# The low parts of eight weight pieces made by a negated copy on ScalarE and an accumulating transfer

## The chip, the cores and the metric

The kernel runs on one core of one Trainium2 chip. A core has TensorE (PE), VectorE (DVE), ScalarE (ACT), GpSimd (POOL) and SyncE (SP), each with a queue of its own that it works through in order, and DMA engines that all queues share. The metric is the device time of one execution in microseconds; less is better. Before the change it is 1096.87 us, the median of three runs (1096.74 to 1097.33).

## The reference

The reference is a network of two layers on 256 tokens with 1024 features, in float32. Each layer has a feed-forward block, a mixer and another feed-forward block; every one is normed, modulated by a vector c, and added to x. The first layer's mixer is the hybrid: a gated linear recurrence (LRU) beside a state-space part (SSD).

```python
for layer in range(DEPTH):
    mod = (c_act @ ada_w[layer] + ada_b[layer]).reshape(bsz, N_SUB, 3, D_MODEL)[:, :, :, None, :]
    ...
    h = modulate(x, 0)
    x = x + HALF_STEP * (1.0 + mod[:, 0, 2]) * swiglu(h, ffn_w_gate[layer, 0], ffn_w_up[layer, 0], ffn_w_down[layer, 0])
    h = modulate(x, 1)
    if layer % 2 == 0:
        ...
        y = hybrid_mixer(h, hyb_w_in[e], hyb_w_out[e], lru_conv_w[e], lru_conv_b[e], ...)
    else:
        ...
        y = mlstm_block(h, mlstm_w_up[o], ...)
    x = x + (1.0 + mod[:, 1, 2]) * y.astype(x.dtype)
    ...
return rms_norm(x, final_norm_g)
```

In the hybrid, `h @ w_in` gives five parts: the gate and the input of the LRU, and z, xbc and dt of the SSD. A causal convolution of width 4 runs over the LRU's input and over xbc. The outputs of both parts are put beside each other and multiplied by `w_out`.

## The kernel before

**Weights as a stream of pieces.** All large weights lie in DRAM as one list of 128x128 tiles in the order in which TensorE uses them, eight tiles to a piece: 366 pieces of 128x1024 in float32, 512 KB each. TensorE multiplies in a rounded format (float32r), so a weight is split into a high part, the rounded weight, and a low part, what the rounding left out; the activations are split the same way. A product is then three matmuls: high weight by high activation (L443), high by low (L444), low by high (L445). In `begin`, which starts a block ahead of its norm, the same three are L509 to L511.

**How a piece is made.** `_piece` (L91 on) loads the raw piece by a transfer of SP (L95), lets ACT round it to `whi` by a copy (L101), and DVE subtract to give `wlo` (L102). Edges of the form "in order" keep ACT's copies in the order of the pieces, and DVE's subtractions too. `behind` sets a piece's copy or subtraction behind another instruction; in the hybrid this concerns pieces 70 to 72. `W.last` is the newest subtraction; `pump` (L273 on) sets the blocks of the modulation (one transfer of SP and one DVE instruction of 128x1024 each, L260 and L262) behind it.

**Buffers.** There are four raw buffers. `whi` and `wlo` have three places each by the piece's number modulo 3, two buffers to a place, so that a piece's parts go where those of the piece six earlier were. `next` makes pieces four ahead of the one that TensorE begins (`LEAD`).

**The hybrid.** It is made of pieces 66 to 119. Pieces 66 to 69 are the first four chunks of xbc, 70 to 77 its other eight (`xbc_pair`, `xbc_rest`); from 78 to 95 a loop takes, by turns, eight tiles of the LRU's input (`xl`), eight of z and two for the LRU's gates (`ri`); 96 to 103 are the LRU's gate (`gl`), and 104 to 119 the output (`od`). Each product fills one of four PSUM banks, which must be read out before it is filled again. For xbc and xl the convolution does that: its first tap by ACT (L730), the other three by DVE (L733). For z, ACT takes a tanh and DVE reads the bank once more (L949, L950); for `ri`, ACT reads both halves (L920, L922).

The SSD's sum runs beside the products of `gl`. For each of four pairs of chunks ACT makes decays (L983, L985, and an exponential, L986), DVE multiplies them (L988, L992), and TensorE uses them (L1008). Twice the norm of four chunks is found from a sum over tokens (L359) and a chain of eight small steps of DVE (L373 to L329) whose end is spread by TensorE (L405).

**What sets the order.** The order of each engine's instructions is the scheduler's of the framework: by priority in the order of the program, with the timing that it assumes, and bound by the edges written by hand. It is fixed when the kernel is built. POOL issues a few small loads and fills a few tiles; in the hybrid its last instructions are two fills (L846, L849) at 192 us.

Of the kernel before, what the change touches and what calls it, by code (L numbers as in the profile page):

```python
# [11 lines left out]
F32 = mybir.dt.float32  # L12
F32R = mybir.dt.float32r
I32 = mybir.dt.int32
AF = mybir.ActivationFunctionType
ALU = mybir.AluOpType
AX = mybir.AxisListType
NOSYNC = mybir.DependencyInfo(mybir.DependencyClass.NoSync, mybir.DependencyReason.DATA)
# [45 lines left out]
WARM = 3  # L64
SUMS = {"n1": (1, 11), "n2": (2, 11), "n4": (4, 14)}
WHOLE = 2


ADA_PLAN = [
# [5 lines left out]
class Weights:  # L75
# [4 lines left out]
    def __init__(self, tc, src, raw_pool, part_pool, pump):  # L80
        self.tc, self.nc, self.src, self.pump = tc, tc.nc, src, pump
        self.raw_pool, self.part_pool = raw_pool, part_pool
        self.pos = 0
        self.made = 0
        self.ahead = 0
        self.parts = {}
        self.products = []
        self.splits = {}
        self.after = {}

    def _piece(self, i):  # L91
        nc = self.nc
        w = PIECE * P
        raw = self.raw_pool.tile([P, w], F32, tag="wraw", name=f"wraw{i}")
        nc.sync.dma_start(raw, self.src[i])  # L95
        if i < WHOLE:
            self.parts[i] = (raw, None)
            return
        hi, lo = (self.part_pool.tile([P, w], F32R, tag=f"{n}{'abc'[i % 3]}", name=f"{n}{i}") for n in ("whi", "wlo"))
        with self.tc.high_priority(offset=self.ahead):  # L100
            raw_hi = nc.scalar.copy(hi, raw)  # L101
            self.last = nc.vector.tensor_tensor(out=lo, in0=raw, in1=hi.bitcast(F32), op=ALU.subtract)  # L102
        if i < 2:
            self.tc.add_manual_dep(self.last.ins, self.first.ins.name, NOSYNC, reason="the first input first")
        self.parts[i] = (hi, lo)
        self.splits[i] = (raw_hi, self.last)
        if i - 1 in self.splits:
            for n in range(2):
                self.tc.add_manual_dep(self.splits[i][n].ins, self.splits[i - 1][n].ins.name, NOSYNC, reason="in order")
        for n, ins in self.after.pop(i, ()):  # L110
            self._behind(i, n, ins)

# [1429 lines left out]
```

## Time and profile before

| what | value |
|---|---|
| median of three runs | 1096.87 us |
| the profiled execution | 1097.25 us |
| its span, first to last instruction | 1095.5 us |
| granted TensorE clock | 0.999 |
| DVE, ACT and POOL busy | 920.5, 639.5 and 8.8 us |
| moved by DMA | 272.34 MB |
| of it by POOL's queue | 1.04 MB in 400 packets |

A row of a group says the line, the engine and the operation, what it writes and reads by the program's names, its shape and count, then busy time, the mean of one in ns, the idle time of the engine just ahead of it and what ended that. A timeline row begins with the start in us from the span's start and the duration. A matmul's row shows 276 ns, but matmuls overlap in the array: how fast TensorE goes is seen from one start to the next. A hole in TensorE's work is therefore read from start to start too; the idle time that the row gives is shorter.

### The profile page before, as it was taken

The numbers are of one execution on the slowest core, as the hardware profiler recorded it, in microseconds if no ns is written. First come the engines' busy times: TensorE is split into PE (matmuls) and PEld (weight loads), VectorE is DVE, ScalarE is ACT, GpSimd is POOL, SyncE is SP. The second block draws the span as 40 slices with busy tenths as digits, with TensorE's granted clock in tenths as the row PEclk, the third lists the DMA queues.
The fourth block names the chain that finished last, engine by engine and source line by source line (L and its number), as shares of the span: only waits on it lengthen the run. The fifth ranks groups of instructions, "written<-read, shape, count | busy, mean of one in ns | idle before, by whom it ended". The sixth has DMA issues, their size and how long they took to land.

```text
span 1095.5 us, 23272 instructions
## 1 busy us (share of the span) xinstructions
PE 1083.8 (99%) x9315; PEld 1070.4 (98%) x9315; DVE 920.5 (84%) x1654; ACT 639.5 (58%) x1053; POOL 8.8 (1%) x28
## 2 busy tenths in 40 slices
PE   9999999999999999999999999999999999999997
PEld 7999999999999999999999999999999999999997
DVE  7999999899999899989698798979768868866552
ACT  5765555678986564554454455448776655544452
POOL 0000000000000000000000000010000000000000
PEclk9999999999999999999999999999999999999999
DMA  9889999556855489999848799963432664875551
GB/s 375 344 318 391 387 352 343 178 196 195 279 167 191 139 307 370 354 351 327 281 142 323 266 356 346 338 204 119 146 102 81 208 193 137 298 239 193 193 174 39
DMA packets 75534, 272.34 MB, mean 249 GB/s; under 512 B 8593, under 2 KB 9393, under 8 KB 75426
## 3 DMA queue, kind: packets, MB, share of 16 engines
q1 hardware_dynamic: 74592, 269.38, 69.7%
q8 instruction: 73, 1.20, 0.4%
q0 software_dynamic: 400, 1.04, 0.4%
q10 hardware_dynamic: 434, 0.43, 0.1%
q14 instruction: 35, 0.29, 0.1%
HBM read 269.77 MB, written 1.05 MB: 247 GB/s over the span
## 4 chain that ended last, share of the span: by engine, by line
PE 80%; DVE 12%; DMA 4%; issue 2%; ACT 1%; ACTq 0%; DVEq 0%; SPq 0%
PE gu L445 12%; PE gu L444 12%; PE gu L443 11%; PE od L445 10%; PE od L443 10%; PE od L444 10%; DVE wlo L102 4%; DMA wraw<-in_wst_dram 3%; PE zz L445 1%; PE zz L443 1%; PE zz L444 1%; DMA wgr<-in_ml_wg_dram 1%; DVE ada L262 1%; DVE xc L733 1%; PE gu_f L509 1%
## 5 line engine op out<-in xcount | busy, mean ns | idle before, releaser
L102 DVE TENSOR_TENSOR wlo<-wraw,whi 128x1024 fp32r<-128x1024 f32 x364 | 442.9, 1221 | 83.6 <-ACT whi L101 83.0
L101 ACT CAST whi<-wraw 128x1024 fp32r<-128x1024 f32 x364 | 378.2, 1050 | 210.9 <-DMA wraw<-in_wst_dram 80.2
L444 PE MATMUL gu<-hb,whi 128*128 128x256 f32 x1296 | 358.0, 276 | 0.4 <-DVE hb L668 0.3
L443 PE MATMUL gu<-hb,whi 128*128 128x256 f32 x1296 | 358.0, 276 | 0.0
L445 PE MATMUL gu<-hb,wlo 128*128 128x256 f32 x1296 | 357.9, 276 | 0.1
L444 PEld LDWEIGHTS gu<-hb,whi 128*128 128x128 f32 x1296 | 243.3, 188 | 0.8 <-DVE hb L668 0.8
L445 PEld LDWEIGHTS gu<-hb,wlo 128*128 128x128 f32 x1296 | 243.3, 188 | 0.2 <-DVE wlo L102 0.2
L443 PEld LDWEIGHTS gu<-hb,whi 128*128 128x128 f32 x1296 | 243.2, 188 | 0.0
L443 PE MATMUL od<-ph,whi 128*128 128x256 f32 x704 | 194.3, 276 | 0.0
L444 PE MATMUL od<-ph,whi 128*128 128x256 f32 x704 | 194.3, 276 | 0.0
L445 PE MATMUL od<-ph,wlo 128*128 128x256 f32 x704 | 194.3, 276 | 0.0
L262 DVE SCALAR_TENSOR_TENSOR ada<-ada,cact 128x1024 f32<-128x1024 f32 x144 | 175.3, 1218 | 1.4 <-DMA ada<-in_adaT_dram 1.3
L444 PEld LDWEIGHTS od<-ph,whi 128*128 128x128 f32 x704 | 132.1, 188 | 0.0
L445 PEld LDWEIGHTS od<-ph,wlo 128*128 128x128 f32 x704 | 132.1, 188 | 0.0
L443 PEld LDWEIGHTS od<-ph,whi 128*128 128x128 f32 x704 | 132.1, 188 | 0.0
L426 ACT CAST ph<-fg 128x256 fp32r<-128x256 f32 x88 | 35.1, 406 | 114.9 <-DVE fg L595 114.9
L427 DVE TENSOR_TENSOR ph<-fg,ph 128x256 fp32r<-128x256 f32 x88 | 36.4, 421 | 14.2 <-ACT ph L426 14.2
L416 ACT ACTIVATE sq_o<-x 128x256 f32<-128x256 f32 x42 | 17.5, 418 | 45.6 <-DVE x L571 40.6
L571 DVE SCALAR_TENSOR_TENSOR x<-od,gate,x 128x256 f32<-128x256 f32 x48 | 23.1, 481 | 24.4 <-PE od L445 24.2
L444 PE MATMUL zz<-hb,whi 128*128 128x256 f32 x128 | 36.2, 283 | 0.0
L445 PE MATMUL zz<-hb,wlo 128*128 128x256 f32 x128 | 36.1, 282 | 0.0
L443 PE MATMUL zz<-hb,whi 128*128 128x256 f32 x128 | 35.8, 279 | 0.0
(431 smaller groups left out, 1959.1 us busy)
## 6 DMA issues: line engine op xcount, KB each, us to landing
wraw<-in_wst_dram SPq DMA_DIRECT2D x366, 512.0 KB, 4.6
ada<-in_adaT_dram SPq DMA_DIRECT2D x144, 512.0 KB, 5.6
xn<-in_x_dram SPq DMA_DIRECT2D x2, 512.0 KB, 4.0
wgr<-in_ml_wg_dram POOLq DMA_DIRECT2D x3, 256.0 KB, 5.4
out_dram<-res SPq DMA_DIRECT2D x3, 128.0 KB, 2.4
out_dram<-res ACTq DMA_DIRECT2D x1, 256.0 KB
out_dram<-res SPq DMA_DIRECT2D x1, 256.0 KB, 2.9
cols<-in_cols_dram SPq DMA_DIRECT2D x1, 190.0 KB, 9.5
```

What stands on the lines that cost most here:

```text
L101: raw_hi = nc.scalar.copy(hi, raw)
L102: self.last = nc.vector.tensor_tensor(out=lo, in0=raw, in1=hi.bitcast(F32), op=ALU.subtract)
L262: return nc.vector.scalar_tensor_tensor(out=raw, in0=raw, scalar=1.0, in1=cact, op0=ALU.mult, op1=ALU.mult, accum_out=mods[s][:, m:m + 1])
L416: square = nc.scalar.activation(q, x, AF.Square).ins
L426: nc.scalar.copy(hi, src)
L427: nc.vector.tensor_tensor(out=both[:, 1, :], in0=src, in1=hi.bitcast(F32), op=ALU.subtract)
L443: m = nc.tensor.matmul(dst, wh, both[:, 0, :], start=start, stop=False, skip_group_check=True)
L444: W.products += [m, nc.tensor.matmul(dst, wh, both[:, 1, :], start=False, stop=False, skip_group_check=True), nc.tensor.matmul(dst, wl, bo ...
L445: nc.tensor.matmul(dst, wl, both[:, 0, :], start=False, stop=stop, skip_group_check=True)]
L509: W.products += [nc.tensor.matmul(dst, wh, rh, start=(k == 0), stop=False), nc.tensor.matmul(dst, wh, rl, start=False, stop=False), nc.ten ...
L571: nc.vector.scalar_tensor_tensor(out=xs_t[d], in0=dst, scalar=g[:, d:d + 1], in1=xs_t[d], op0=ALU.mult, op1=ALU.add)
L733: nc.vector.scalar_tensor_tensor(out=dst[:, o:], in0=src[:, :T - o], scalar=cw(j), in1=dst[:, o:], op0=ALU.mult, op1=ALU.add)
```

## The change

For eight pieces of the hybrid (75, 78, 81, 84, 87, 90, 93 and 106) the low part is no longer made by DVE. ACT, after the rounded copy, writes the rounded piece with the opposite sign into `wlo`: a copy with scale -1 of the raw piece, rounded to the same format. Then POOL issues a transfer that reads the raw piece from DRAM once more and adds it to what stands in `wlo`. The result is again raw less rounded.

For these pieces `W.last` stays the subtraction before, and the edge "in order" of DVE goes from that subtraction to the next piece that has one. The edge among ACT's rounded copies goes through all pieces as before; the negated copies have no such edge. The two lines on `i < 2` that are taken out did nothing, since pieces 0 and 1 leave the function before.

```diff
+ADDED = (75, 78, 81, 84, 87, 90, 93, 106)
...
+        self.last = None
...
+        added = i in ADDED
         with self.tc.high_priority(offset=self.ahead):
             raw_hi = nc.scalar.copy(hi, raw)
-            self.last = nc.vector.tensor_tensor(out=lo, in0=raw, in1=hi.bitcast(F32), op=ALU.subtract)
-        if i < 2:
-            self.tc.add_manual_dep(self.last.ins, self.first.ins.name, NOSYNC, reason="the first input first")
+            if added:
+                low = nc.scalar.activation(lo, raw, AF.Copy, scale=-1.0)
+                nc.gpsimd.dma_start(lo, self.src[i].bitcast(F32R), accum_op=ALU.add)
+            else:
+                low = nc.vector.tensor_tensor(out=lo, in0=raw, in1=hi.bitcast(F32), op=ALU.subtract)
         self.parts[i] = (hi, lo)
-        self.splits[i] = (raw_hi, self.last)
-        if i - 1 in self.splits:
-            for n in range(2):
-                self.tc.add_manual_dep(self.splits[i][n].ins, self.splits[i - 1][n].ins.name, NOSYNC, reason="in order")
+        if self.splits:
+            self.tc.add_manual_dep(raw_hi.ins, self.splits[max(self.splits)][0].ins.name, NOSYNC, reason="in order")
+        if added:
+            self.splits[i] = (raw_hi, self.last)
+            return
+        if self.last is not None:
+            self.tc.add_manual_dep(low.ins, self.last.ins.name, NOSYNC, reason="in order")
+        self.last = low
+        self.splits[i] = (raw_hi, low)
         for n, ins in self.after.pop(i, ()):
             self._behind(i, n, ins)
```

## The prediction

> **What bounds the kernel now.** I read the page first, then stretches of 20 us, then what TensorE waited for, then TensorE's rows at those places.
>
> ```profile
> span 1095.5 us, 23272 instructions
> PE 1083.8 (99%) x9315; PEld 1070.4 (98%) x9315; DVE 920.5 (84%) x1654; ACT 639.5 (58%) x1053; POOL 8.8 (1%) x28
> ...
> L102 DVE TENSOR_TENSOR wlo<-wraw,whi 128x1024 fp32r<-128x1024 f32 x364 | 442.9, 1221 | 83.6 <-ACT whi L101 83.0
> L101 ACT CAST whi<-wraw 128x1024 fp32r<-128x1024 f32 x364 | 378.2, 1050 | 210.9 <-DMA wraw<-in_wst_dram 80.2
> ```
>
> TensorE (PE) is busy for 99% of the span, so no edit on another engine can give more than PE's few holes. The pair that the change edits are the last two rows: ScalarE (ACT) rounds a piece, then VectorE (DVE) subtracts, 364 times each.
>
> ```profile
> 220.00:240.00 20.00, 19.73 (x174) 19.56 (x173) 18.75 (x38) 14.72 (x27) 0.00 (x0) 1.00 0.57 193
> ...
> 260.00:280.00 20.00, 20.00 (x173) 19.52 (x172) 19.94 (x38) 15.66 (x30) 0.00 (x0) 1.00 0.70 232
> 280.00:300.00 20.00, 18.31 (x166) 17.53 (x165) 20.00 (x35) 19.71 (x47) 0.00 (x0) 1.00 0.85 287
> ...
> 320.00:340.00 20.00, 19.19 (x166) 18.82 (x165) 19.76 (x41) 15.87 (x22) 0.00 (x0) 1.00 0.29 93
> 340.00:360.00 20.00, 20.00 (x179) 20.00 (x178) 18.44 (x29) 12.21 (x17) 0.00 (x0) 1.00 0.73 251
> ```
>
> The columns are the length, then PE, weight load, DVE, ACT and POOL, each busy time with its number of instructions, then the granted clock and the DMA share. A full stretch holds 179 matmuls, one per 0.112 us. In the hybrid PE loses some: 280 to 300 has 166 matmuls and 18.31 us busy while DVE is busy for all of it and ACT for 19.71. PE's rows (start, duration, what; idle time before and who ended it) show the holes:
>
> ```profile
> 220.24 0.28 PE L445 MATMUL xbc<-hb,wlo 128*128 128x256 f32 x1
> 220.79 0.36 PE L443 MATMUL xbc<-hb,whi 128*128 128x256 f32 x1 [0.28 <-DVE ssd_x L733]
> ...
> 282.85 0.28 PE L445 MATMUL ri<-xlb,wlo 128*128 128x256 f32 x1
> 283.90 0.39 PE L443 MATMUL z<-hb,whi 128*128 128x256 f32 x1 [0.77 <-DVE lru_x L733]
> ...
> 295.28 0.28 PE L443 MATMUL gl<-hb,whi 128*128 128x256 f32 x1
> 296.41 0.66 PE L1008 MATMUL y<-mt,ssd 128*64 128x128 f32 x8 [0.85 <-DVE mt L988]
> ...
> 330.61 0.28 PE L445 MATMUL od<-ysb,wlo 128*128 128x256 f32 x1
> 331.61 0.57 PE L405 MATMUL rsb_g<-ident,rsy_g 128*128 128x128 f32 x3 [0.72 <-DVE rsy_g L329]
> ```
>
> From start to start, less 0.11 for a matmul, the four holes are 0.44, 0.94, 1.02 and 0.89 us: 3.3 us in all. Each is ended by DVE. That is the ceiling of the gain, 0.30% of the time. About 0.2% (2.2 us) is what a measurement of this kernel can tell from no change, so the question is how many holes close.
>
> **The change on DVE.** Eight subtractions go. In rows of DVE, those that lie just ahead of the holes are these (the first row holds pieces 74 and 75, the second and third are 90 and 93):
>
> ```profile
> 216.33 2.36 DVE L102 TENSOR_TENSOR wlo<-wraw,whi 128x1024 fp32r<-128x1024 f32 x2
> 218.60 2.43 DVE L733 SCALAR_TENSOR_TENSOR ssd_x<-xbc,cols,ssd_x 128x255 f32<-128x255 f32 x6
> ...
> 259.11 1.22 DVE L102 TENSOR_TENSOR wlo<-wraw,whi 128x1024 fp32r<-128x1024 f32 x1
> ...
> 270.63 1.22 DVE L102 TENSOR_TENSOR wlo<-wraw,whi 128x1024 fp32r<-128x1024 f32 x1
> ...
> 283.37 0.48 DVE L733 SCALAR_TENSOR_TENSOR lru_x<-xl,cols,lru_x 128x253 f32<-128x253 f32 x1
> ```
>
> One subtraction holds DVE for 1.14 us to the next start (2.36 less 1.22), so eight free 9.1 us of DVE, of which only the part ahead of a hole counts. Hole 1: the convolution from 218.60 releases the PSUM bank that PE waits for; without piece 75 it can start 1.14 us sooner, more than 0.44, so the hole closes. Hole 2: DVE works without a pause that matters from 260 to 284 (19.94 of 20 us in the row above), and 90 and 93 lie in that stretch, so the L733 of 283.37 can come 2.28 us sooner; the hole of 0.94 closes. Hole 4: the subtraction of piece 106, the last edited one, stands well ahead of it (first row), and DVE waits for PE in between (second row), so its 1.14 us are given back there:
>
> ```profile
> 311.07 1.22 DVE L102 TENSOR_TENSOR wlo<-wraw,whi 128x1024 fp32r<-128x1024 f32 x1
> ...
> 319.55 0.87 DVE L1012 SCALAR_TENSOR_TENSOR ssd_x<-ssd_x,cols,y 128x256 f32<-128x256 f32 x2 [0.40 <-PE y L1008]
> ```
>
> I count nothing for hole 4.
>
> **The change on ACT.** Eight copies with scale -1 are added. No such copy of 128x1024 stands in the trace; the cast of that shape is 1.05 us (L101 above) and the exponential of that shape 1.14 (L986 below), so 1.05 each, 8.4 us in all. It cannot be under zero, since an instruction is added and none removed on ACT. In the stretches of 220 and 260 above ACT has 5.3 and 4.3 us free of 20, and I take each copy as hidden there; without that cover it would be up to 1.05 us on whatever ACT does next. Hole 3 is where ACT decides:
>
> ```profile
> 279.45 0.28 PE L445 MATMUL ri<-xlb,wlo 128*128 128x256 f32 x1
> ...
> 280.76 0.47 ACT L920 ACTIVATE lru_aq<-ri,hb 128x256 f32<-128x256 f32 x1
> ...
> 293.63 1.14 ACT L986 ACTIVATE mt<-mt 128x1024 f32<-128x1024 f32 x1
> ...
> 295.13 1.22 DVE L988 TENSOR_TENSOR mt<-mt,cbt 128x1024 f32<-128x1024 f32 x1
> ```
>
> From 280.76 to the exponential ACT has almost no pause, so this run of work moves only as far as its head moves. The head reads a bank that PE finishes at about 279.6, and 0.44 earlier once hole 1 is closed: about 279.2, plus some 0.1 to be released. So ACT can shift by 1.4 us at most. DVE then begins L988 as ACT ends (about 293.3) instead of 295.13, and y starts about 1.8 us sooner, at 294.6. PE itself would arrive 0.44 + 0.94 sooner, so of the 1.02 us of hole 3 some 0.6 stay and 0.4 go. On its end nothing but these three sums is on the path: 0.44 + 0.94 + 0.4 = 1.8 us.
>
> **The change on the queues.** POOL gets eight transfers. The stretches above show 0.00 for it, so its wait for ACT's copy delays no other work. SP's loads of raw pieces are still waiting for buffers; an added piece frees its buffer with ACT's copy instead of the later subtraction, so they go out earlier, and 4.2 MB more are moved. TensorE gets the new wait: the first product with the low part now needs the transfer's landing. The trace of before holds no accumulating transfer. The nearest rows are POOL's plain loads of 256 KB (first) and SP's raw pieces of 512 KB in the hybrid (second), each min, median and max:
>
> ```profile
> DMA to landing us min/median/max: 3.0/5.4/6.7
> ```
>
> ```profile
> DMA to landing us min/median/max: 3.3/4.1/5.5
> ```
>
> The lower bound is 3.3: as quick as the fastest raw piece of its size. The upper is 12.2: the slowest of POOL's loads and on top the slowest raw piece, since an accumulation must fetch the destination besides the source. I take 6, near POOL's own median, as the hybrid's DMA share is 0.57 to 0.70 ahead of 280. What there is time for, by pieces 75, 78 and 84:
>
> ```profile
> 214.83 1.03 ACT L101 CAST whi<-wraw 128x1024 fp32r<-128x1024 f32 x1
> 221.07 1.05 ACT L101 CAST whi<-wraw 128x1024 fp32r<-128x1024 f32 x1 [1.06 <-DMA wraw<-in_wst_dram]
> 238.84 1.99 ACT L101 CAST whi<-wraw 128x1024 fp32r<-128x1024 f32 x2
> ```
>
> ```profile
> 223.83 0.28 PE L445 MATMUL xbc<-hb,wlo 128*128 128x256 f32 x1
> ```
>
> ```profile
> 233.35 0.28 PE L445 MATMUL xl<-hb,wlo 128*128 128x256 f32 x1
> ```
>
> ```profile
> 249.69 0.28 PE L445 MATMUL z<-hb,wlo 128*128 128x256 f32 x1
> ```
>
> Piece 75: cast done at 215.86, negated copy at 216.9 if it follows at once, first use at 223.83 less the 0.44 that PE gains: 6.5 us. Piece 78 has 233.35 - 0.44 - 223.2 = 9.7, and 84, the first of its row's two casts, 249.69 - 0.44 - 240.9 = 8.3. With 6 us none is late, 75 by a hair.
>
> [...]
>
> **The sum.** The profiled execution is 1097.25 us with a span of 1095.5, and lies 0.38 above the median of 1096.87. 1097.25 - 1.8 = 1095.45; against the median 1095.1.
>
> **The rivals.** *All holes close.* The scheduler sets the order on each engine anew, and with eight subtractions gone L986 or the small root steps ahead of L329 may come earlier than in my count. For it speaks that DVE is full at every hole; against it ACT's 19.71 of 20 us at hole 3, and that nothing edited stands ahead of hole 4. All four closed give 1096.87 - 3.3 = 1093.6; the first three, 2.4, suffice for more than 0.2%.
>
> *The transfer lands late: slower.* At piece 75 PE waits for the landing time less 6.5 us; what PE is late there also shifts the head of ACT's run, so the change is landing time - 6.5 - 1.8. It breaks even at 8.3 us, is slower by over 0.2% from 10.5, and at 12.2 gives 1100.8. PE being late then gives the later pieces as much more time, so I count it once. [...] Against it: the median of 5.4, the low DMA share there. [...]
>
> *ACT takes DVE's place.* If the added copies are not hidden, DVE waits for rounding and for the first tap of the convolutions instead. Only hole 1 closes: 1096.87 - 0.44 = 1096.4. For it: ACT at 14.7 to 15.7 of 20 us already; against: it has idle time right after most casts.
>
> **How the numbers follow.** My forecast (holes 1 and 2, part of 3) has 0.36, with its own range of 1094.7 to 1096.0. More holes closed has 0.34, ACT 0.08, the late landing 0.22, of which 0.03 lie within the 0.2%. So faster 0.34, same 0.36 + 0.08 + 0.03 = 0.47, slower 0.19. The range runs from 1093.4 (all holes, with the slow first matmul after each) to 1099.5, a landing time of 10.9 us; beyond lies about 0.15.
>
> **What would show it.** Right: 356 subtractions on DVE; no PE idle time at L733 near 220 and 283; a y start after a shorter wait for DVE mt; the wait for rsy_g still there; landing of POOL's transfers of 5 to 7 us. Wrong: a PE wait for a DMA into wlo at L445, above all at piece 75; ACT's negated copies much over 1.05 us; PE holes that stay although DVE has idle time ahead of them.

## The result, and the profile after

The changed kernel takes 1104.42 us (median of four runs, 1104.24 to 1104.86), the kernel before beside it 1096.88 (1096.74 to 1097.33). The ratio is 1.0069, with a 95% interval of 1.0051 to 1.0086: slower, where 1095.1 had been forecast. The profiled execution took 1104.55 us, 7.3 more than that of before, and its span is 6.8 longer. These are lines of its page (the span, the busy times, the two groups of the weights' parts, and a line of the DMA issues: form, count, KB each, median us to landing). Line numbers of the changed kernel are 2 to 10 higher than before (L101 is now L104, L102 is L109, L443 is L453).

```profile
span 1102.3 us, 23293 instructions
PE 1086.2 (99%) x9315; PEld 1072.3 (97%) x9315; DVE 913.6 (83%) x1646; ACT 646.3 (59%) x1061; POOL 15.7 (1%) x36
...
L104 ACT CAST whi<-wraw 128x1024 fp32r<-128x1024 f32 x364 | 379.3, 1051 | 220.5 <-DMA wraw<-in_wst_dram 80.3
L109 DVE TENSOR_TENSOR wlo<-wraw,whi 128x1024 fp32r<-128x1024 f32 x356 | 433.2, 1221 | 90.2 <-ACT whi L104 89.4
...
wlo<-in_wst_dram POOLq DMA_DIRECT2D x8, 512.0 KB, 9.1
```

The change does what it says: 356 subtractions are left and eight transfers are new. But a transfer's median to its landing is 9.1 us, where 6 had been taken. What TensorE waited for (us in total, times, the longest) shows where this strikes:

```profile
PE xbc L455 <- DMA wlo<-in_wst_dram: 3.2, 1, 3.2
PE idle L213 <- POOL ident masks.py:199: 1.6, 1, 1.6
PE od L453 <- ACT ysb L436: 1.4, 1, 1.4
PE ab L984 <- ACT ce L995: 0.8, 1, 0.8
PE rsb_g L415 <- DVE rsy_g L339: 0.7, 1, 0.7
PE y L1018 <- DVE mt L998: 0.5, 1, 0.5
```

The waits for L733 of before (now L743) are gone, so holes 1 and 2 are closed. In their place stand a wait for a transfer, one for ACT's copy of `ysb` near the end of the hybrid, and one for ACT's `ce` right ahead of the third hole. The second line, at the start of the program, is in both kernels. The transfer's wait in rows, first POOL's, then TensorE's:

```profile
217.10 0.89 POOL L107 DMA_DIRECT2D wlo<-in_wst_dram  x1 [24.52 <-ACT ssd L800]
```

```profile
223.23 0.28 PE L454 MATMUL xbc<-hb,whi 128*128 128x256 f32 x1
226.72 0.39 PE L455 MATMUL xbc<-hb,wlo 128*128 128x256 f32 x1 [3.22 <-DMA wlo<-in_wst_dram]
...
228.22 0.42 PE L454 MATMUL xbc<-hb,whi 128*128 128x256 f32 x1
228.43 0.41 PE L455 MATMUL xbc<-hb,wlo 128*128 128x256 f32 x1
```

Piece 75 is issued at 217.10 and TensorE goes on at 226.72. And the wait is not all: from 228 on a matmul begins every 0.21 us and no longer every 0.11. The stretches (length; PE, weight load, DVE, ACT and POOL busy with their counts; granted clock, DMA share, GB/s) say why:

```profile
224.57:227.99 3.42, 1.27 (x10) 1.27 (x11) 1.76 (x4) 2.16 (x4) 0.49 (x1) 1.00 1.03 386
227.99:231.40 3.41, 3.41 (x18) 3.41 (x17) 1.89 (x3) 1.83 (x3) 0.00 (x0) 0.50 1.05 261
```

For 3.41 us after the wait TensorE has a granted clock of 0.50: 18 matmuls lie in that stretch, and 32 in the next one of its length, where the clock is whole again.

**Where the time came from.** Number all matmuls in the order in which they ran, in both traces, take each number's start in the changed kernel less its start before, and watch this lag grow from stage to stage. Up to the hybrid it is 0.0. Hole 1 takes 0.5 off, piece 75 adds 5.2 (3.4 for the wait, 1.6 while the clock is halved, the rest just after the wait), nothing changes up to the second hole, which takes 1.1 off. The third hole adds 0.6, the stretch from 300 to 322 adds 0.8, that from 322 to 346 (the output's products, with hole 4) 2.0, and what follows -0.3: 6.8 in all. The rows behind the 2.0 are these, of TensorE, DVE and ACT:

```profile
337.76 0.68 PE L415 MATMUL rsb_g<-ident,rsy_g 128*128 128x128 f32 x4 [0.73 <-DVE rsy_g L339]
...
340.80 0.73 PE L453 MATMUL od<-ysb,whi 128*128 128x256 f32 x4 [1.43 <-ACT ysb L436]
```

```profile
336.32 1.22 DVE L109 TENSOR_TENSOR wlo<-wraw,whi 128x1024 fp32r<-128x1024 f32 x1
337.46 0.16 DVE L339 SCALAR_TENSOR_TENSOR rsy_g<-rsw_g,rsy_g 128x2 f32<-128x2 f32 x1
...
338.71 1.20 DVE L109 TENSOR_TENSOR wlo<-wraw,whi 128x1024 fp32r<-128x1024 f32 x1
339.83 1.26 DVE L973 SCALAR_TENSOR_TENSOR ssd_x<-ssd_x,cols,rsb_g 128x256 f32<-128x256 f32 x3
```

```profile
339.29 1.04 ACT L104 CAST whi<-wraw 128x1024 fp32r<-128x1024 f32 x1 [1.36 <-PE od L454]
340.34 1.58 ACT L436 CAST ysb<-ssd_x 128x256 fp32r<-128x256 f32 x4
```

The same place in the kernel before, in rows of DVE and then of ACT:

```profile
331.33 0.14 DVE L329 SCALAR_TENSOR_TENSOR rsy_g<-rsw_g,rsy_g 128x2 f32<-128x2 f32 x1
331.38 1.22 DVE L102 TENSOR_TENSOR wlo<-wraw,whi 128x1024 fp32r<-128x1024 f32 x1
332.52 1.65 DVE L963 SCALAR_TENSOR_TENSOR ssd_x<-ssd_x,cols,rsb_g 128x256 f32<-128x256 f32 x4
```

```profile
333.03 0.80 ACT L426 CAST ysb<-ssd_x 128x256 fp32r<-128x256 f32 x2 [0.29 <-DVE ssd_x L963]
```

The spread of the root (`rsb_g`) now stands 13 matmuls later in TensorE's order. On DVE a subtraction stands ahead of the root's last step, which it did not before. Between that step and the scaling (L973, before L963) there was one subtraction; now two scans (L1067) stand there besides, so the scaling starts 2.4 us after the step and not 1.2. On ACT a rounded copy stands ahead of the copies of `ysb`. So `ysb` is late. Nobody wrote that order: the scheduler made it when piece 106 lost its subtraction, and where 106 keeps it (e2, e3 and e7 below) TensorE's order behind 318 us is that of before.

The 0.8 between 300 and 322 is order too. TensorE's products `y` have 64 columns (128*64 in the row), the products around them 128. From one start to the next a change between the two forms takes 0.20 us, a 128*128 product after another 0.11, a 128*64 product after another 0.055 in the mean. Before, the `y` of this stretch stand in three unbroken blocks, so there are 6 changes. Now one block is split by `rsb_g` and another by products of `gl`, and there are 10. In all 18 profiled executions the same 209 starts, up to the first products of `od`, take 20.8 to 20.9 us with 6 changes, 21.4 with 8 (e15; in e9 TensorE waits there besides) and 21.8 with 10.

### The profile page after: what moved, and what is told of

Its sections match the earlier page's. It is cut to its first block, busy times and chain, and to the rows that moved or that the text cites. A ratio compares the mean times of both kernels' runs of the same rounds, so it can differ in the third digit from the quotient of the medians.

```text
span 1102.3 us, 23293 instructions
## 1 busy us (share of the span) xinstructions
PE 1086.2 (99%) x9315; PEld 1072.3 (97%) x9315; DVE 913.6 (83%) x1646; ACT 646.3 (59%) x1061; POOL 15.7 (1%) x36
## 3 DMA queue, kind: packets, MB, share of 16 engines
HBM read 273.97 MB, written 1.05 MB: 249 GB/s over the span
## 4 chain that ended last, share of the span: by engine, by line
PE 88%; DVE 6%; DMA 2%; ACT 2%; issue 1%; ACTq 0%; DVEq 0%
PE gu L454 13%; PE gu L453 13%; PE gu L455 13%; PE od L454 10%; PE od L455 10%; PE od L453 10%; DVE wlo L109 2%; PE zz L455 1%; PE zz L453 1%; PE zz L454 1%; PE gu_f L519 1%; PE gu_f L521 1%; PE gu_f L520 1%; DMA wraw<-in_wst_dram 1%; DMA wlo<-in_wst_dram 1%; DVE xc L743 1%
## 5 line engine op out<-in xcount | busy, mean ns | idle before, releaser
L104 ACT CAST whi<-wraw 128x1024 fp32r<-128x1024 f32 x364 | 379.3, 1051 | 220.5 <-DMA wraw<-in_wst_dram 80.3
L109 DVE TENSOR_TENSOR wlo<-wraw,whi 128x1024 fp32r<-128x1024 f32 x356 | 433.2, 1221 | 90.2 <-ACT whi L104 89.4
L453 PE MATMUL gu<-hb,whi 128*128 128x256 f32 x1296 | 358.0, 276 | 0.0
L453 PEld LDWEIGHTS gu<-hb,whi 128*128 128x128 f32 x1296 | 243.2, 188 | 0.0
L453 PE MATMUL od<-ph,whi 128*128 128x256 f32 x704 | 194.3, 276 | 0.0
L453 PEld LDWEIGHTS od<-ph,whi 128*128 128x128 f32 x704 | 132.1, 188 | 0.0
L453 PE MATMUL zz<-hb,whi 128*128 128x256 f32 x128 | 35.8, 280 | 0.0
```

What stands on the lines that cost most here:

```text
L109: low = nc.vector.tensor_tensor(out=lo, in0=raw, in1=hi.bitcast(F32), op=ALU.subtract)
L453: m = nc.tensor.matmul(dst, wh, both[:, 0, :], start=start, stop=False, skip_group_check=True)
```

## The experiments

Two theories stood at the start. A: one late landing at piece 75, the halved clock after it, and the order that was changed by 106. B: each transfer costs the same, 7.5 / 8 = 0.94 us, wherever it stands. The table shows each kernel's median, its profiled execution and the lag of that execution by the stages just used ("start" is up to 205 us, where no kernel is changed, and where the lag differs by up to 1.0 from one execution to the next; "rest" is from 346 us on). The lags are worked out as above. The kernel before, run beside them, had medians of 1097.9 (e1 to e4), 1097.4 (e5 to e8), 1097.3 (e9 to e12) and 1097.4 us (e13 to e16).

| kernel | median | profiled | start | hole 1 | piece 75 | 78 to 93 | hole 2 | hole 3 | 300 to 322 | 322 to 346 | rest | all |
|---|---|---|---|---|---|---|---|---|---|---|---|---|
| after | 1104.4 | 1104.5 | 0.0 | -0.5 | +5.2 | 0.0 | -1.1 | +0.6 | +0.8 | +2.0 | -0.3 | +6.8 |
| e1 | 1103.9 | 1101.2 | +0.1 | -0.1 | +0.3 | +1.0 | -1.1 | +0.9 | +0.8 | +2.0 | -0.3 | +3.7 |
| e2 | 1102.7 | 1103.4 | +0.3 | -0.5 | +6.7 | 0.0 | -1.1 | +0.2 | 0.0 | 0.0 | +0.5 | +6.0 |
| e3 | 1102.8 | 1100.8 | +0.9 | 0.0 | +0.3 | +1.0 | -0.7 | +1.1 | 0.0 | 0.0 | +0.7 | +3.4 |
| e4 | 1100.3 | 1100.7 | +1.0 | -0.5 | +3.9 | 0.0 | -1.1 | -0.2 | +0.3 | -0.2 | +0.3 | +3.4 |
| e5 | 1101.5 | 1101.8 | +0.5 | -0.5 | 0.0 | +0.8 | -0.7 | +1.1 | +0.8 | +2.0 | 0.0 | +4.0 |
| e6 | 1100.8 | 1100.9 | 0.0 | -0.5 | 0.0 | 0.0 | -1.1 | +0.8 | +0.8 | +3.6 | 0.0 | +3.6 |
| e7 | 1098.6 | 1099.7 | +0.9 | -0.1 | 0.0 | 0.0 | +0.4 | +1.0 | 0.0 | 0.0 | +0.1 | +2.4 |
| e8 | 1100.5 | 1102.2 | +0.3 | 0.0 | 0.0 | 0.0 | -0.3 | 0.0 | +0.8 | +3.6 | +0.5 | +4.9 |
| e9 | 1101.7 | 1100.2 | +0.1 | +1.2 | 0.0 | +0.5 | 0.0 | -0.6 | +2.3 | -0.2 | -0.2 | +2.9 |
| e10 | 1097.7 | 1097.7 | +0.3 | -0.5 | 0.0 | 0.0 | -0.8 | +1.1 | 0.0 | 0.0 | +0.4 | +0.5 |
| e11 | 1098.1 | 1099.4 | +0.1 | 0.0 | 0.0 | 0.0 | -0.2 | 0.0 | 0.0 | -1.0 | +3.2 | +2.1 |
| e12 | 1099.1 | 1097.9 | +0.1 | -0.5 | 0.0 | 0.0 | -0.7 | +1.1 | 0.0 | -1.0 | +1.7 | +0.6 |
| e13 | 1097.7 | 1097.5 | 0.0 | -0.5 | 0.0 | 0.0 | -1.1 | -0.2 | +1.8 | -0.3 | +0.5 | +0.3 |
| e14 | 1098.0 | 1098.0 | 0.0 | 0.0 | 0.0 | 0.0 | -0.4 | -1.0 | +1.8 | -0.2 | +0.6 | +0.8 |
| e15 | 1097.7 | 1097.7 | +0.6 | -0.5 | 0.0 | 0.0 | -1.1 | +0.6 | +0.8 | -0.2 | +0.4 | +0.5 |
| e16 | 1099.4 | 1098.4 | +0.5 | 0.0 | 0.0 | +0.7 | -1.1 | -0.1 | +1.8 | -0.2 | -0.4 | +1.1 |

**e1 to e4: parts of the list alone.**

```diff
-ADDED = (75, 78, 81, 84, 87, 90, 93, 106)
+ADDED = (78, 81, 84, 87, 90, 93, 106)   (e1)
+ADDED = (75, 78, 81, 84, 87, 90, 93)    (e2)
+ADDED = (78, 81, 84, 87, 90, 93)        (e3)
+ADDED = (75,)                           (e4)
```

> Piece 75 is subtracted by VectorE again, the other seven stay as changed. Theory A (one late landing at piece 75: 3.4 us of waiting, then 1.7 us at half the granted clock; a rearranged order around piece 106 costs the rest): no wait for the transfer, the granted clock stays at 1.0, 1104.4 - 5.1 + 0.4 = 1099.7 us. Theory B (every added piece costs about the same through ScalarE's and the DMA's load, 7.5 us over eight): 1103.5 us.

Measured 1103.86 us (ratio 1.0050, interval 1.0035 to 1.0065).

> Piece 106 is subtracted by VectorE again, the other seven stay as changed. Theory A: the wait at 75 and the half clock stay, the holes between 312 and 343 us go back to those of before: 1104.4 - 2.7 = 1101.7 us. Theory B: 1103.5 us.

Measured 1102.74 (1.0041, 1.0028 to 1.0054).

> Pieces 75 and 106 are subtracted by VectorE again, six are left (78 to 93). Theory A: 1104.4 - 5.1 + 0.4 - 2.7 = 1097.0 us, no TensorE wait for a transfer into wlo. Theory B: 1096.9 + 6 x 0.94 = 1102.5 us.

Measured 1102.78 (1.0052, 1.0033 to 1.0070).

> Only piece 75 is made by the negated copy and the transfer. Theory A: the wait of some 3.4 us and the half clock come with it, hole 1 closes: 1096.9 + 5.1 - 0.4 = 1101.6 us. Theory B: 1097.8 us.

Measured 1100.28 (1.0020, 1.0011 to 1.0030).

Neither theory gives all of these times. B is within 0.8 us of the medians of e1, e2 and e3 and misses e4 by 2.5; A misses e1 by 4.2 and e3 by 5.8 (of which 1.0 is in the kernel before, which was that much longer here). In the profiles A's places are right: 75 costs 3.9 to 6.7 us wherever it is in the list (in e2 the clock stays halved for twice as long), and the late stage costs 2.0 only with 106. What A missed is seen in e1 and e3, which are dearer than it said. Without the delay at 75 TensorE comes early enough to find other landings late: that of piece 78 by 0.3 (in the table this stands under piece 75), and that of piece 84:

```profile
PE z L455 <- DMA wlo<-in_wst_dram: 0.7, 1, 0.7
```

And the third hole grows by about 1 in both. B is out in spite of its medians, since no transfer costs its 0.94: the one of e4 costs 2.4 us (3.4 in its profile, less the 1.0 of the start), the one of e8 below 3.1, and the three of e7 together 1.2. The medians of e1 and e3 lie 2 to 3 us above their profiled executions, which the table does not explain. In e1 the three longer executions have a granted clock of 0.997 where the profiled one has 0.998; in e3 the two longest have 0.998 and 0.999, so there the clock is not the reason, and it stays open.

**e5: the same transfers without accumulation. e6: no transfer.**

```diff
-                nc.gpsimd.dma_start(lo, self.src[i].bitcast(F32R), accum_op=ALU.add)
+                nc.gpsimd.dma_start(lo, self.src[i].bitcast(F32R))     (e5)
+                pass                                                   (e6)
```

> All eight transfers stay, but they no longer accumulate: the raw piece is copied over the low part, so the addition is left out and the low part is the raw piece. Every wait and the order of the instructions are those of the change. Theory A (the accumulating transfer lands late, 7.8 to 10.7 us after GpSimd's issue; TensorE then stands still at piece 75, and the granted clock is halved for 3.4 us after that; the rest is the rearranged order at the piece 106 and near the third hole): a plain transfer lands in 6 to 7.5 us, TensorE waits at 75 for 1 us or less and no half clock follows, so the time is 1104.4 - 3.3 + 0.5 - 1.7 = 1099.9 us, 1099 to 1101. Theory B (each transfer costs about the same 0.94 us wherever it stands, by GpSimd's work and the load on the memory): still 1104 us, since eight transfers of the same bytes are there.

Measured 1101.49 (1.0043, 1.0027 to 1.0058); these are, from the page of DMA queues and from the view of the transfer's line, first the changed kernel, then e5:

```profile
q0 software_dynamic: 1552, 5.23, 2.5%
```

```profile
DMA to landing us min/median/max: 7.8/9.1/10.7
```

```profile
q0 software_dynamic: 1552, 5.23, 1.5%
```

```profile
DMA to landing us min/median/max: 4.6/6.5/7.4
```

The same packets and bytes take 2.5% of the DMA engines' span with the addition and 1.5% without, of which 0.4% are the other loads of this queue (from the same line of before). So the eight transfers' packets take 2.1% with the addition and 1.1% without, and the landing is 2.6 us later at the median. With 6.5 TensorE waits for no low part at all, and the clock stays whole at 75: the table's 5.2 becomes 0.0. That is A's cause for piece 75, taken away alone. What is left lies at the start (0.5), at the later stages, and between 78 and 93 (0.8): there, at 244 us, TensorE waits for `xlb`, whose cast stands on ACT behind a negated copy and a rounded one. The median is 0.5 above A's range.

> The negated rounded copy stays on ScalarE and VectorE is relieved of the eight subtractions, but no transfer follows: the addition is left out, and the low part is the negated rounded copy. The order of the other engines is nearly that of the change. Theory A: no late landing and no half clock; what is left is the rearranged order and ScalarE's eight more copies (+0.7 at the third hole, +0.5 after it, +2.2 to +2.7 at the piece 106) less the closed holes 1 and 2 (-1.4): 1096.9 + 2.3 = 1099.2 us, 1098.3 to 1100. Theory B: the transfers are the cost, so without them the time is the forecast's 1095 to 1096 us.

Measured 1100.80 (1.0029, 1.0019 to 1.0038), 0.8 above A's range and far above B's. Without any transfer, hole 1 and hole 2 close as forecast (-1.6 together) and the kernel is still slower. The third hole and what follows take back 5.2, of which the late stage has 3.6. The clock explains why that is more than the 2.0 of e5 with the same order:

```profile
333.85:337.26 3.41, 1.67 (x12) 1.26 (x11) 3.41 (x8) 2.61 (x5) 0.00 (x0) 1.00 0.74 239
337.26:340.67 3.41, 3.41 (x18) 3.41 (x18) 3.41 (x7) 0.62 (x1) 0.00 (x0) 0.50 0.12 47
```

**e7: three pieces with more time. e8: 106 alone.**

```diff
+ADDED = (87, 91, 94)   (e7)
+ADDED = (106,)         (e8)
```

> Added pieces are only 87, 91 and 94, which TensorE needs late enough that a landing of 10.7 us is in time by the places that the trace of the change shows, and 106 keeps its subtraction. Theory A: TensorE waits for no low part, the second hole closes (-0.9) or stays, the third grows by at most 0.7: 1096 to 1097.6 us, so no difference to speak of. Theory B: 3 x 0.94 = 2.8 us slower, 1099.7 us.

Measured 1098.60 (1.0006, 0.9996 to 1.0015): no difference to speak of, and 1.0 above A's range. In the profile the wait of the second hole for L743 is gone, but two others stand just ahead of it: 0.5 from start to start for the landing of 94, which took 9.7 us and had been thought to be in time, and 0.9 for DVE's second reading of z (L960). So the stage grows by 0.4.

> The added piece is 106 alone. Theory A (this piece alone rearranges the end: its subtraction's place goes to the next pieces, which come ahead of the norm's rows on VectorE, and ScalarE's second copy goes ahead of its copies of y): 2.2 to 2.7 us in the last stage and nothing else, 1099.1 to 1099.6 us, with TensorE's waits for ScalarE's L436 in the profile. Theory B: 0.94 us, 1097.8 us.

Measured 1100.53 (1.0028, 1.0016 to 1.0040). One transfer for which TensorE never waits costs 4.4 us between 300 and 346 in its profile, 1.6 of that by a halved clock at 337.7. So 106 hurts without a late landing, and DVE's and ACT's rows at this place are in the order shown above for the changed kernel. ACT's second copy alone is not the cause there: ACT waits 2.4 us for TensorE at 321.9, between that copy (310.6) and the late copies of `ysb` (336.2), and so gives its 1.07 back. With the halved clock, which A had not put there, the median is 0.9 above its range.

**e9: a wait without a transfer.** DVE subtracts three times for piece 75.

```diff
-            self.last = nc.vector.tensor_tensor(out=lo, in0=raw, in1=hi.bitcast(F32), op=ALU.subtract)
+            for _ in range(3 if i == 75 else 1):
+                self.last = nc.vector.tensor_tensor(out=lo, in0=raw, in1=hi.bitcast(F32), op=ALU.subtract)
```

> The kernel before with no transfer at all; VectorE makes the subtraction of piece 75 three times over (2.3 us more of work at the first hole), so TensorE waits there some 2.7 us in place of 0.44. Theory A (the halved clock after a wait belongs to TensorE's standing still for 2 us and more, whatever it waits for): the granted clock is 0.5 for 3.4 us after the wait, which costs 1.7 us; with the wait's 2.3 us and less 0.9 that the second hole gives back the time is 3 us more than before. Rival (the halved clock comes from the transfers, by the load that they put on the core): no half clock, 1.4 to 2.3 us more than before.

Measured 1101.73 (1.0042, 1.0028 to 1.0056). That is above both theories. It tells nothing of the clock: the scheduler spread the three among the convolution's steps, the longest wait in its hybrid is 1.4 us, and the clock stays whole. Its profiled execution was its fastest; why the others were up to 2.2 us longer is not known (their granted clock is 0.999, as in the profiled one). That it takes a wait of 2 us and more, as theory A has it, no run shows: in e11, below, the clock is halved after one of 1.39 us.

**e10 to e12: the holes closed by order alone, no transfer.** An edge sets a subtraction behind the step that releases the bank.

```diff
+BEHIND = {(1, 12): 75, (7, 8): 97}
...
+        if (i, n) in BEHIND:                      (in conv; end is its last step: e10, e12)
+            W.behind(BEHIND[i, n], 1, end)
...
-                if g == 0:
-                    group_norm(0)
+                if g == 0: group_norm(0)          (e11, e12)
+                else: W.behind(109, 1, rsqrt_ends[-1])
```

> The kernel before, with two edges and no transfer: VectorE's subtraction of piece 75 is set behind the convolution that frees the bank of the first hole, and that of 97 behind the convolution at the second. Theory A (the second hole's gain runs into ScalarE's full queue at the third hole, as in the runs with the change): holes 1 and 2 close, the third grows by about 1 us; 0.2 to 0.6 us less than before. Rival (what the change gained at the holes was lost to ScalarE's eight second copies alone): 1.4 us less than before.

Measured 1097.74 (1.0002, 0.9993 to 1.0010). TensorE's order is row for row that of before. Holes 1 and 2 give 1.3 and the third hole takes 1.1 of it back. In rows, TensorE's, then ACT's:

```profile
294.03 0.50 PE L975 MATMUL ab<-stk,sel 128*128 128x256 f32 x2 [0.80 <-ACT ce L986]
296.48 0.66 PE L1009 MATMUL y<-mt,ssd 128*64 128x128 f32 x8 [0.76 <-DVE mt L989]
```

```profile
293.79 1.14 ACT L987 ACTIVATE mt<-mt 128x1024 f32<-128x1024 f32 x1
```

The exponential, at 293.63 before, is at 293.79. Less the start lag of 0.3 it comes 0.1 us sooner, where TensorE comes 1.3 sooner. Two rows of ACT say why, first before, then e10:

```profile
279.53 1.06 ACT L101 CAST whi<-wraw 128x1024 fp32r<-128x1024 f32 x1 [0.91 <-DMA wraw<-in_wst_dram]
...
283.88 0.41 ACT L426 CAST xlb<-lru_x 128x256 fp32r<-128x256 f32 x1 [0.23 <-DVE lru_x L733]
```

```profile
279.44 1.05 ACT L101 CAST whi<-wraw 128x1024 fp32r<-128x1024 f32 x1 [0.74 <-DMA wraw<-in_wst_dram]
...
282.60 0.41 ACT L426 CAST xlb<-lru_x 128x256 fp32r<-128x256 f32 x1 [0.61 <-DVE lru_x L732]
```

The head of ACT's run (280.76 before, 280.67 in e10) comes, on ACT, right behind a rounded copy that waits for its raw piece to land, so it is only 0.4 sooner (less the start lag). And inside the run ACT waits 0.61 for DVE's convolution where it waited 0.23, because the scheduler now sets the cast of `xlb` ahead of a rounded copy that stood ahead of it before.

> The kernel before, with one edge and no transfer: VectorE's subtraction of piece 109 is set behind the end of the norm's chain of the second group, so the fourth hole (0.89 us) should close, and nothing is late behind it, since no second copy stands ahead of ScalarE's copies of y. Theory A: 0.9 us less than before. Rival (VectorE's full queue gives the hole back at the next copies of y, as it did when 106 was added): no difference, or up to 1 us more.

Measured 1098.07 (1.0013, 1.0004 to 1.0022), 0.8 above the kernel before: the rival's time, at another place. The fourth hole closes, and the gain of 1.0 stands until the next block's norm, where TensorE waits longer than it had gained and the clock is halved, in a kernel that has no accumulating transfer:

```profile
368.96 0.61 PE L359 MATMUL rst_n<-ones,sq_o 128*128 128x1 f32 x4 [1.39 <-ACT sq_o L416]
```

```profile
367.48:370.89 3.41, 2.02 (x17) 1.93 (x17) 2.10 (x9) 0.81 (x2) 0.15 (x1) 1.00 0.47 142
370.89:374.30 3.41, 3.41 (x18) 3.41 (x17) 1.89 (x6) 0.33 (x1) 0.00 (x0) 0.50 0.12 26
```

> The edges of both, no transfer. Theory A: 1.1 to 1.5 us less than before; the rival for the first two edges: 2.3 us less. This is the version that the experiments point to as one that could beat both kernels.

Measured 1099.11 (1.0021, 1.0012 to 1.0030): slower, in neither theory's range. Its lags are those of e10 and e11 side by side, without the halved clock; its profiled execution lies 1.2 below the median.

**e13 to e16: ACT relieved ahead of the third hole.** Rounded copies of pieces 100 and 101 go behind the exponential.

```diff
+            end = nc.scalar.activation(mt, mt, AF.Exp, scale=-1.0)
+            if m0 == 0: W.behind(100, 0, end); W.behind(101, 0, end)    (e15: 101 alone)
...
+ADDED = (78, 81, 87, 90, 93)                                            (e16)
```

> The edges of e10, and the rounded copies of pieces 100 and 101 (1.05 us each on ScalarE, at 286 and 288 us) set behind the exponential at the third hole, which needs neither. Theory A (ScalarE's full queue ends the third hole): the exponential starts up to 2.1 us earlier and the third hole shrinks by 1 to 2 us, so the gain of holes 1 and 2 is kept: 1.0 to 2.0 us less than before. Rival (VectorE's queue or the chain through TensorE ends it): the time is that of e10, no difference.

Measured 1097.69 (1.0006, 0.9997 to 1.0015).

```profile
291.39 1.14 ACT L987 ACTIVATE mt<-mt 128x1024 f32<-128x1024 f32 x1
```

```profile
293.85 0.66 PE L1009 MATMUL y<-mt,ssd 128*64 128x128 f32 x8 [1.03 <-DVE mt L990]
```

With two copies less the exponential comes 2.40 us sooner than in e10, `y` 2.63 sooner (0.3 of each lies in the start), and the third hole's stage goes from +1.1 to -0.2. So ACT's run of work ended that hole, as A has it. The time is the rival's all the same, because 1.8 are given back between 300 and 322. TensorE's rows there:

```profile
316.64 0.43 PE L1009 MATMUL y<-mt,ssd 128*64 128x128 f32 x2
317.00 0.71 PE L405 MATMUL rsb_g<-ident,rsy_g 128*128 128x128 f32 x4
317.64 0.54 PE L1009 MATMUL y<-mt,ssd 128*64 128x128 f32 x5
...
320.02 0.39 PE L443 MATMUL od<-ysb,whi 128*128 128x256 f32 x2
320.86 0.39 PE L444 MATMUL od<-ysb,whi 128*128 128x256 f32 x1 [0.45 <-DVE ysb L427]
```

> The kernel before with only the two rounded copies set behind the exponential; holes 1 and 2 stay as they were. Theory A: the third hole (1.02 us and the 0.5 us ahead of it) shrinks, 0.7 to 1.5 us less than before. Rival: no difference.

Measured 1097.95 (1.0003, 0.9995 to 1.0012): the third hole gives 1.0, the next stage takes 1.8.

> As e13, but only the rounded copy of piece 101 is set behind the exponential: half of the work is taken from ahead of it. Theory A: 0.5 to 1.2 us less than before. Rival: no difference.

Measured 1097.72 (1.0006, 0.9998 to 1.0015): no difference either.

> The change with the pieces 78, 81, 87, 90 and 93 only (without 75 and 84, which TensorE waited for, and without 106, which rearranges the end), and with the two rounded copies of e13 set behind the exponential. Theory A: hole 2 closes (0.9 us), the third hole keeps that, TensorE waits for low parts by at most 0.5 us: from 1 us less than before to no difference. Rival (each transfer costs some 0.5 to 0.9 us by itself): 2.5 us more or worse.

Measured 1099.40 (1.0017, 1.0008 to 1.0026). The third hole is held (-0.1), hole 2 closes, and TensorE waits for no low part. The change still loses: 1.8 between 300 and 322, and 0.7 at a product of z, where TensorE waits for a small step of DVE (L853).

The 1.8 us have two parts in e13, e14 and e16. The new edges let the scheduler break the blocks of `y`, as 106 did: there are 10 changes of form and not 6, for 0.9 us. The other 0.9 lies at the first products of `od`: in e13 TensorE comes there 0.8 us sooner than before, waits for `ysb`, and leaves at the time of before. No run takes the two parts apart. No version here beats the kernel before.

## Why the prediction was wrong

The forecast was 1.8 us less; in the profiles it was 6.8 more. Of the 8.6 between them, by the stages of the table, 5.2 lie at piece 75, 1.0 at hole 3, 2.8 at the order around piece 106, and -0.4 in the rest.

**Hole 1 and hole 2: right.** "0.44 + 0.94" were 0.5 and 1.1 in the changed kernel, and e6 shows them without a transfer. ACT's eight copies took 1.07 us in the mean (1.05 to 1.15) where 1.05 had been taken, and no wait of TensorE in the changed kernel is put down to one; in e5 they delay `xlb`.

**The landing: the step that failed first.** "I take 6, near POOL's own median" is right for a plain transfer (6.5 in e5) and wrong for an accumulating one (9.1, from 7.8 to 10.7). The text gives a reason itself, in its upper bound: the destination must be fetched besides the source. That is an argument from what an addition does, and no run shows it: e5 shows that the addition costs the time, and not which part of its work. With 9.6 us for piece 75, against the 6.5 that there was time for, the wait should be 3.1, and 3.2 was measured; so the budget was right.

**The price of lateness: "landing time - 6.5 - 1.8".** With 9.6 that rival gives 1.3 us slower, and it was 7.5. It left out the halved clock, 1.6 us of the 5.2 at piece 75. "I count it once" held in the changed kernel, but not because the others had time enough: e1 shows that 78 and 84 are late as soon as 75 is not.

**Hole 3: "some 0.6 stay and 0.4 go".** It grew by 0.6. The prediction let ACT come up to 1.4 us sooner, as the head of its run waits for TensorE's bank and the run has almost no pause. e10 shows 0.1: the head stands behind a rounded copy that waits for a raw piece, and the run got a longer wait for DVE. e10 has no second copy, so these copies are not needed for it. That ACT's run ends the hole was right, as e13 shows by taking work out of it. This means also that closing holes 1 and 2 could not pay by itself: in e10 both close, and the time is that of before.

**Hole 4: "I count nothing", and the order.** The subtraction's time is given back as said and the wait for `rsy_g` is still 0.7. But taking a piece out of the chain of "in order" edges let the scheduler set the next ones elsewhere: 0.8 us by the broken blocks of `y` and 2.0 by the late `ysb`. The prediction had named the scheduler only as a way to gain.

**The ceiling of 3.3 us** was no sum of gains to be had. Each experiment that closed a hole found its time again further on: at hole 3 after 1 and 2 (e10), at the wait for `ysb` and in a new order of `y` after 3 (e13, e14), at the next norm after 4 (e11). That fits a reading by which TensorE's holes are where it catches up with DVE and ACT, which are nearly full there (at hole 3, from 280 to 300 us before, 20.00 and 19.71 of 20 us); but part of the loss in e13 and e14 is order alone, so it is not the whole account.

## What to carry to other kernels

Here an accumulating transfer of 512 KB took 1.4 times as long to land as a plain one (9.1 us at the median, against 6.5): measure one before work that TensorE waits for is set on it. Where TensorE is 99% busy and two other engines are full at its holes, add up what these engines do from one hole to the next, before a hole is booked as a gain. And an edit that takes an instruction out of a chain of order edges also edits the order of everything that the scheduler sets by it; compare the new order with the old before costing the edit.

## What the runs showed of the hardware

**After a wait the granted clock was halved, in six of 18 profiled executions.** Inside the work this is seen in after, e2, e4, e6, e8 and e11, behind waits of which the longest were 3.2, 3.5, 2.0, 1.4, 1.4 and 1.4 us. The clock was 0.50 for 3.41 us (after, e4, e6, e11); in e8 it was 0.59 in the mean from 337 to 341 us, and in e2 0.84 from 214 to 236, which is about twice 3.41 us at half. In the 3.41 us ahead of that TensorE was busy for 1.27 us in after, 1.39 in e4, 1.67 in e6 and 2.02 in e11: 37, 41, 49 and 59%. This share alone did not decide it: 1.60 us of 3.41 in e1 (from 334.03 us) and 1.84 in e12 were not followed by a halved clock. The stretches of e12, with a longer wait than e11's (1.9 against 1.4):

```profile
365.76:369.17 3.41, 1.84 (x16) 1.63 (x14) 2.99 (x8) 1.89 (x6) 1.06 (x2) 1.00 0.77 228
369.17:372.58 3.41, 3.11 (x26) 3.12 (x27) 2.23 (x11) 0.64 (x2) 0.00 (x0) 1.00 0.13 50
```

The halved clock cost 1.6 us at piece 75 of the changed kernel, and 1.6 in e6 and in e8 (3.6 where e5 has 2.0). In the changed kernel it began 218.45 us after the clock had first been granted in that execution (9.53 to 227.99), which is 64 times 3.413 us; in the kernel before, the clock goes down at the end, 1082.03 us after the first grant (10.43 to 1092.46), 317 times 3.413. The first grant so differed by 0.9 us between the two. That the same wait can for this reason be followed by a halved clock in one execution and not in another, and that some of these kernels spread over 2 to 5 us by it, is the author's guess. The mean granted clock, which is on record for every execution, agrees for three: in the profiled ones it is 0.998 or 0.999 without a halved clock inside the work, 0.997 or 0.998 with 3.41 us of it and 0.995 in e2, with twice that; in e15 the three executions of 1099.5 us and more have 0.997 and the eight others, of 1098.5 and less, 0.998 or 0.999; e11 is split in the same way at 1099, and in e12 7 of 11 have 0.997 or less. It does not account for e3 and e9, which spread over 4.5 and 2.2 us at 0.998 to 0.999.

**A change between products of 64 and of 128 columns took TensorE longer than a further product of the same form.** It took 0.20 us from start to start, against 0.11 between two of 128*128 and 0.055 between two of 128*64 (the first 209 starts after 300 us before; the changed kernel shows the same). Why it took this long is not shown. A new order with four more of them took 0.9 us longer.

**The accumulating transfers held the DMA engines about twice as long as the plain ones** (2.1% of their span for 4.2 MB in the changed kernel, 1.1% in e5), and in the changed kernel their instructions held POOL for 0.85 to 0.89 us each, where the plain ones took 0.53. Which part of the later landing belongs to which was not tried.
